# A relative-position table made in the first stage and spread over its rows head by head, DRAM to DRAM

## The chip, the cores and the metric

The kernel runs on one core of a Trainium2 chip. The metric is the time on the device in microseconds (us), from the start of the program to its end. The core has five engines that each run their own instruction stream in order: TensorE (PE in the profile, with PEld for its weight loads), VectorE (DVE), ScalarE (ACT), GpSimd (POOL) and SyncE (SP). SP computes nothing here and issues most DMA transfers; POOL issues the rest. The transfers of both run on 16 shared DMA engines.

## What is computed

One inference step of a hybrid encoder layer, for a prompt of 512 frames and a sample of 64 frames with a cache of 1024 past frames. A projection of 18,032 columns feeds two branches, a gated delta rule over 16 heads and a sparse attention over 16 heads, which are gated, summed and projected back. The change touches only the bias that the attention adds to its logits, which depends on the head and on the distance between key and query:

```python
def sparse_attention(q, qi, wi, q_pos, K, V, KI, topk, rel_bias):
    ...
    rel = top_idx - q_pos[None, :, None]
    bias = rel_bias[rel_bucket(rel)].astype(jnp.float32)
    ...
    logits = jnp.where(valid[:, :, None, None, :], logits + bias, -jnp.inf)
    p = jax.nn.softmax(logits, axis=-1).astype(V.dtype)
```

`rel_bias` has 32 buckets by 16 heads. Distances beyond 128 all fall in one bucket, so a head needs 384 distinct values at most near the diagonal.

## The kernel before

A Python class records the whole program by hand. The weight matrices are cut into **tiles** of 128 columns by 2048 rows; `run_tile` (L314) handles tile n: 64 matmuls with the high part of the weights (`whi`), then 32 with the low part (`wlo`), 96 in all, of 128x288 each. During tile n, `split` (L276) makes `whi` and `wlo` of tile n+1: ACT writes the rounded weights and their negative, then two POOL-issued transfers add the raw weights (`wraw`) onto `wlo` in flight. At the 84th matmul, `load` (L264) has SP issue the 1 MB load of `wraw` for tile n+3; it waits until the transfers that read the buffer's former content have landed.

The program has stages. In the first one (until about 410 us) the first projections, the indexer's scores and the start of the top-k run. Then comes the **delta-rule stage** (until about 1619 us), with four to six tiles for each of its 16 heads: `head_pre(h)` (L1260) opens head h ahead of its key tile. `open_att` (L1775) starts the **attention stage**, two tiles per head (queries `qb`, gate `zb`). Two stages for the output follow.

All work besides the tiles (decays, triangular solve, scan, attention of a head, stores) is written as generators, called tasks. `spawn` starts one; after each matmul of a tile, `tick` (L156) steps each task that is due and so writes its next instructions between the tile's matmuls. When a task is due is decided while the program is written, by a planner that keeps a clock for PE, one for each engine and one for DMA, and a time at which each tensor is ready. On the chip nothing of this clock is left but the order of the instructions on each engine, with waits on semaphores. For a transfer the planner advances its DMA clock by bytes that it works out from the shapes of the operands `aps`:

```python
        for x in aps:
            m = 1
            for s in x.shape[1:]:
                m *= s
            n = max(n, m)
        ...
            by = 4 * n * out.shape[0]
            self.dma = max(self.dma, start + 1500) + by / 360.0
            end = self.dma + 1300
```

A matmul advances the PE clock at least to the time when its operands are ready (`account_pe`, L123), and tasks that wait for a tensor are due when the planner holds it ready.

**The bias.** `bias_setup` (L1278) is a task of the attention stage. It loads three small constants (`oh`, `rb`, `far`), makes the table `f` of 16 heads by 512 distances with one matmul (`biasp`), and writes it to DRAM as `d_F` of 16 x 128 x 384: 128 equal rows for each head, 3 MB in one transfer from 16 partitions. A read of `d_F` at a row pitch of 383 instead of 384 (`toeplitz`, L1301) then gives a head's block of 128 queries by 256 keys, shifted by one from row to row. `attend` (L1340) reads this block into `BT` for its head, once the tasks `kv_load` and `bias_setup` are done; `attend_block` adds it to the logits `lg`, in blocks named `L`. Ahead of the first head, `conv_out` (L1306) transposes four pieces (`nc`), copies them to `ncr` and stores them, and `kv_load` transposes the cached keys (`kst`, `kcp`). `gate_vectors` (L1510) loads `gada`, 64 pieces of 256 KB, through the whole attention stage.

Of the kernel before, what the change touches and what calls it, by code (L numbers as in the profile page):

```python
# [7 lines left out]
F32 = mybir.dt.float32  # L8
# [200 lines left out]
class Kern(Plan):  # L209
# [138 lines left out]
    def consts(self, ctx):  # L348
        nc, tc, i = self.nc, self.tc, self.i
        cp = self.cp = ctx.enter_context(tc.tile_pool(name="cp", bufs=1))  # L350
        self.ident = cp.tile([128, 128], F32, name="ident")
        self.A.dma_start(self.ident, i["k_ident"])
        self.mE = cp.tile([128, 2, 128], F32, name="mE")
        self.ones = cp.tile([128, 1], F32, name="ones")
        self.V.memset(self.ones, 1.0)
        self.pm = ctx.enter_context(tc.tile_pool(name="pm", bufs=3, space=PSUM))
        self.px = ctx.enter_context(tc.tile_pool(name="px", bufs=2, space=PSUM))
        self.pc = ctx.enter_context(tc.tile_pool(name="pc", bufs=2, space=PSUM))
        self.po = ctx.enter_context(tc.tile_pool(name="po", bufs=1, space=PSUM))
        self.dp = ctx.enter_context(tc.tile_pool(name="dp", bufs=1, space=DRAM))  # L360
        dt = self.dp.tile
        self.d_g = dt([16, TX], F32, name="d_g")
        self.d_kT = dt([2, 128, T], F32, name="d_kT")
        self.d_v = dt([T, 256], F32, name="d_v")
        self.d_oa = dt([H, 128, T], F32, name="d_oa")
        self.d_za = dt([H, 128, T], F32, name="d_za")
        self.d_gb = dt([H, 128, T], F32, name="d_gb")
        self.d_t = dt([2, KO, 128, T], F32, name="d_t")
        self.d_ya = dt([KO, 128, T], F32, name="d_ya")
        self.d_F = dt([16, 128, 384], F32, name="d_F")  # L370
        self.d_D = [dt([128, T], F32, name=f"d_D{e}") for e in range(2)]

# [887 lines left out]
    def head_pre(self, h):  # L1260
        def pre():
            if h == 0:
                self.join(self.misc_task)
            if h >= 3:
                self.join(self.heads[h - 3]["scan"])
            st = self.heads[h] = dict(h=h)
            st["dec"] = self.spawn(self.decays(st))
            st["scan"] = self.spawn(self.scan(st))
        return pre
# [7 lines left out]

    def bias_setup(self):  # L1278

        i, p, V, S = self.i, self.p3, self.V, self.S  # L1280
        oh = p.tile([32, 512], F32, tag="L3", name="oh", bufs=1)
        S.dma_start(oh, i["k_onehot"])
        rb = p.tile([32, 16], F32, name="rb", bufs=1)
        S.dma_start(rb, i["rel_bias"])
        self.far = p.tile([128, 16], F32, name="far", bufs=1)
        S.dma_start(self.far, i["rel_bias"][15:16, :].partition_broadcast(128).rearrange("p a b -> p (a b)"))
        yield [oh, rb, self.far], 9000
        ps = yield from self.tr("biasp")
        self.mm(ps[:16, :], rb, oh)
        f = p.tile([16, 512], F32, tag="PT3", name="bf", bufs=1)  # L1290
        V.tensor_copy(f, ps[:16, :])
        self.fars = p.tile([128, 8], F32, name="fars", bufs=1)
        v = self.far.rearrange("p (a b) -> p a b", b=2)
        for s in range(2):
            V.tensor_copy(self.fars[64 * s:64 * s + 64, :], v[64 * s:64 * s + 64, :, s])
        yield [f]

        S.dma_start(self.d_F, f[:, 0:384].unsqueeze(1).to_broadcast([16, 128, 384]))
        yield [self.d_F]

    def toeplitz(self, h, n, w):  # L1301

# [36 lines left out]

    def attend(self, a):  # L1340
        S, p, h = self.S, self.p3, a["h"]
        yield from self.wait(self.kv_task, self.bias_task)
        BT = p.tile([128, 256], F32, tag="BT", name=f"BT{h}")
        S.dma_start(BT, self.toeplitz(h, 128, 256))
        yield [BT, a["qT"], a["zt"]]
        yield from self.wait(*[self.spawn(self.attend_block(a, t, BT)) for t in (3, 2, 1, 0)])
        if h % 2:
            a["sample"] = self.spawn(self.attend_sample(h // 2))
# [426 lines left out]
    def open_att(self):  # L1775
        self.drain()
        self.c2.close()
        self.c3, self.p3 = self.pool("p3")
        self.slack = 0.0
        self.gpool = lambda: self.p3  # L1780
        self.bias_task = self.spawn(self.bias_setup())
        self.spawn(self.conv_out())
        self.spawn(self.gate_vectors())
        self.qb_pre(0)()
# [41 lines left out]
    def run(self):  # L1826
        tc = self.tc
        with ExitStack() as ctx:
            ctx.enter_context(tc.manual_schedule())
            self.consts(ctx)  # L1830
            cp = self.cp
# [3 lines left out]
                setattr(self, n, cp.tile([128, 5, 16], F32, name=n))  # L1835
            self.gate = cp.tile([128, KO, 2], F32, name="gate")
            self.diag = cp.tile([128, 64], F32, name="diag")
            self.ur = cp.tile([128, 32], F32, name="ur")
            self.heads, self.att, self.kvT, self.tok = {}, {}, {}, {}
            self.score_tasks, self.topk_task = [], None  # L1840
# [9 lines left out]
            p = self.p1  # L1850
# [7 lines left out]
            for b in range(2):  # L1858
                q = p.tile([128, 2, 128], F32R, name=f"qss{b}", bufs=1)
                self.V.tensor_scalar(q, self.ident.unsqueeze(1).to_broadcast([128, 2, 128]), 0.0, None, op0=ALU.mult)  # L1860
                self.qss.append(q)
            self.tri = p.tile([128, 2, 128], F32, name="tri", bufs=1)
            self.cache_task = self.spawn(self.cache_idx())
            self.load(3)
            for n in range(2):
# [70 lines left out]
```

## Time and profile before

| | us |
|---|---|
| runs | 3054.83, 3056.27, 3066.11 |
| median of the runs | 3056.27 |
| the profiled execution, its own time | 3063.92 |
| its span in the trace | 3061.8 |

| busy share of the span | |
|---|---|
| PE | 96% |
| PEld | 92% |
| ACT | 50% |
| DVE | 39% |
| POOL | 13% |

The page shows 40 slices of the span. PE is at 9 tenths or more in nearly all of them; the exceptions are the first two, the slices at about 1620 to 1700 us (7 and 8 tenths) and some in the output stages. The DMA engines carry 183 GB/s on average. To read it: PE bounds the kernel nearly everywhere, so a stretch in which PE stands idle can be won, and work elsewhere costs only where PE comes to wait for it.

### The profile page before, as it was taken

The numbers are of one execution on the slowest core, as the hardware profiler recorded it, in microseconds if no ns is written. First come the engines' busy times: TensorE is split into PE (matmuls) and PEld (weight loads), VectorE is DVE, ScalarE is ACT, GpSimd is POOL, SyncE is SP. The second block draws the span as 40 slices with busy tenths as digits, with TensorE's granted clock in tenths as the row PEclk, the third lists the DMA queues.
The fourth block names the chain that finished last, engine by engine and source line by source line (L and its number), as shares of the span: only waits on it lengthen the run. The fifth ranks groups of instructions, "written<-read, shape, count | busy, mean of one in ns | idle before, by whom it ended". The sixth has DMA issues, their size and how long they took to land.

```text
span 3061.8 us, 59253 instructions
## 1 busy us (share of the span) xinstructions
PE 2934.6 (96%) x23931; PEld 2814.4 (92%) x23931; DVE 1204.6 (39%) x3643; ACT 1533.3 (50%) x3428; POOL 391.5 (13%) x776
## 2 busy tenths in 40 slices
PE   6999999999999999999997899999999999999897
PEld 2599999999999999999996899899999899999897
DVE  3344996545455545545531444244412111111112
ACT  3266444556555565555552455355445444444454
POOL 1011111111111111111110001111011111111110
PEclk7999999999999999999998999999999999999999
DMA  9875877677677766676678776777769998888875
GB/s 330 272 160 128 198 184 182 157 163 161 160 163 161 164 159 153 151 172 153 156 160 172 167 169 166 182 169 169 167 152 255 236 232 220 208 215 214 222 160 141
DMA packets 572387, 558.81 MB, mean 183 GB/s; under 512 B 54865, under 2 KB 467426, under 8 KB 570898
## 3 DMA queue, kind: packets, MB, share of 16 engines
q1 hardware_dynamic: 517826, 357.81, 41.3%
q0 software_dynamic: 54144, 197.16, 34.0%
q8 instruction: 188, 3.08, 0.4%
q14 instruction: 85, 0.70, 0.1%
q10 hardware_dynamic: 144, 0.07, 0.0%
HBM read 310.37 MB, written 47.45 MB: 117 GB/s over the span
## 4 chain that ended last, share of the span: by engine, by line
PE 82%; DMA 9%; DVE 3%; ACT 3%; SPq 2%; issue 1%; POOL 0%; ACTq 0%; DVEq 0%; POOLq 0%
PE mm L221 67%; SPq L58 2%; DMA za<-d_za 1%; DMA wlo<-wraw 1%; PE ada L221 1%; PE ob L221 1%; DMA gbl<-d_gb 1%; PE lg L221 1%; PE mmp L221 1%; PE dot L221 1%; PE po L221 1%; DMA xf<-in_x_sample 1%; DMA wa<-in_w_ada 1%; ACT whi L58 1%; ACT wlo L58 1%
## 5 line engine op out<-in xcount | busy, mean ns | idle before, releaser
L221 PE MATMUL mm<-hh,whi 128*128 128x288 f32 (+1 forms) x4448 | 1217.2, 300 | 4.8 <-ACT gth L58 4.5
L221 PE MATMUL mm<-hl,whi 128*128 128x288 f32 (+1 forms) x4448 | 1215.9, 300 | 0.0
L221 PEld LDWEIGHTS mm<-hh,whi 128*128 128x128 f32 (+1 forms) x4448 | 837.8, 188 | 14.0 <-ACT gth L58 5.3
L221 PEld LDWEIGHTS mm<-hl,whi 128*128 128x128 f32 (+1 forms) x4448 | 837.8, 188 | 7.9 <-issue 3.8
L221 PE MATMUL mm<-hh,wlo 128*128 128x288 f32 (+1 forms) x4448 | 683.0, 302 | 4.5 <-DMA wlo<-wraw 4.5
L221 PEld LDWEIGHTS mm<-hh,wlo 128*128 128x128 f32 (+1 forms) x4448 | 615.6, 190 | 6.6 <-DMA wlo<-wraw 4.7
L58 POOL DMA_DIRECT2D wlo<-wraw x376 | 324.0, 862 | 2313.2 <-ACT wlo L58 1926.8
L58 ACT ACTIVATE whi<-wraw 128x512 fp32r<-128x512 f32 x756 | 467.4, 619 | 98.1 <-DMA wraw<-in_w_branch_b 63.1
L58 ACT ACTIVATE wlo<-whi 128x512 fp32r<-128x512 f32 x752 | 475.2, 632 | 76.4 <-PE mm L221 35.9
L221 PE MATMUL mm<-ga,whi 128*128 128x288 f32 x1024 | 142.4, 299 | 7.5 <-DVE ta L58 7.5
L221 PEld LDWEIGHTS mm<-ga,whi 128*128 128x128 f32 x1024 | 139.7, 192 | 8.4 <-DVE ta L58 8.4
L221 PE MATMUL mm<-mg,whi 128*128 128x288 f32 x1024 | 143.6, 297 | 0.0
L221 PE MATMUL mm<-gb,whi 128*128 128x288 f32 x1024 | 138.8, 296 | 0.3 <-DVE tb L58 0.3
L221 PEld LDWEIGHTS mm<-mg,whi 128*128 128x128 f32 x1024 | 138.2, 189 | 0.0
L221 PEld LDWEIGHTS mm<-gb,whi 128*128 128x128 f32 x1024 | 136.8, 188 | 0.6 <-DVE tb L58 0.5
L58 DVE SCALAR_TENSOR_TENSOR cv<-raw,cw,cv 128x579 f32<-128x579 f32 x144 | 117.8, 818 | 33.6 <-ACT cv L58 30.4
L58 DVE SCALAR_TENSOR_TENSOR gacc<-gada,cs,gacc 128x512 f32<-128x512 f32 x120 | 86.7, 744 | 30.9 <-DMA gada<-in_w_ada 30.8
L58 ACT ACTIVATE raw<-mm 128x288 f32<-128x288 f32 x96 | 36.8, 383 | 87.4 <-PE mm L221 86.6
L58 ACT ACTIVATE gth<-mm 128x288 f32<-128x288 f32 x64 | 25.9, 407 | 108.3 <-PE mm L221 104.6
L58 ACT ACTIVATE x<-px 128x128 f32<-128x128 f32 x80 | 22.0, 275 | 116.0 <-PE px L221 115.6
L58 DVE TENSOR_TENSOR xf<-yp,xf 128x512 f32<-128x512 f32 (+1 forms) x18 | 11.4, 632 | 160.5 <-PE yp L236 133.7
L58 DVE SCALAR_TENSOR_TENSOR tb<-tb,mm 128x288 f32<-128x288 f32 x32 | 14.5, 452 | 143.3 <-DMA tb<-d_t 110.3
(493 smaller groups left out, 3422.8 us busy)
## 6 DMA issues: line engine op xcount, KB each, us to landing
wlo<-wraw POOLq DMA_DIRECT2D x376, 512.0 KB, 5.5
wraw<-in_w_in SPq DMA_DIRECT2D x140, 1024.0 KB
wa<-in_w_ada SPq DMA_DIRECT2D x64, 512.0 KB
gada<-in_w_ada SPq DMA_DIRECT2D x64, 256.0 KB
wraw<-in_w_branch_a SPq DMA_DIRECT2D x16, 1024.0 KB
wraw<-in_w_branch_b SPq DMA_DIRECT2D x16, 1024.0 KB
wraw<-in_w_out SPq DMA_DIRECT2D x16, 1024.0 KB
d_t<-gth SPq DMA_DIRECT2D x32, 288.0 KB
```

The lines of the kernel that those rows point to most:

```text
L58: r = f(*a, **k)
L221: self.nc.tensor.matmul(out, lhsT, rhs, start=start, stop=stop, **k)
```

## The change

Four things change. The table `f` is made by a task of the first stage, from that stage's pool, with `far` and `fars` moved to the pool that lives throughout. What is written to DRAM from it is only `d_f`, 16 rows of 384 (24 KB). The 128 equal rows of a head are now written by `bias_rows(h)`, called in `head_pre(h)`: one transfer from DRAM to DRAM of 192 KB, issued by POOL, whose source is read 128 times. And `attend` no longer waits for the bias task.

```diff
--- before.py
+++ after.py
@@ -367,6 +367,7 @@
         self.d_gb = dt([H, 128, T], F32, name="d_gb")
         self.d_t = dt([2, KO, 128, T], F32, name="d_t")
         self.d_ya = dt([KO, 128, T], F32, name="d_ya")
+        self.d_f = dt([16, 384], F32, name="d_f")
         self.d_F = dt([16, 128, 384], F32, name="d_F")
         self.d_D = [dt([128, T], F32, name=f"d_D{e}") for e in range(2)]
 
@@ -1263,6 +1264,7 @@
                 self.join(self.misc_task)
             if h >= 3:
                 self.join(self.heads[h - 3]["scan"])
+            self.bias_rows(h)
             st = self.heads[h] = dict(h=h)
             st["dec"] = self.spawn(self.decays(st))
             st["scan"] = self.spawn(self.scan(st))
@@ -1277,26 +1279,28 @@
 
     def bias_setup(self):
 
-        i, p, V, S = self.i, self.p3, self.V, self.S
-        oh = p.tile([32, 512], F32, tag="L3", name="oh", bufs=1)
+        i, p, cp, V, S = self.i, self.p1, self.cp, self.V, self.S
+        oh = p.tile([32, 512], F32, name="oh", bufs=1)
         S.dma_start(oh, i["k_onehot"])
         rb = p.tile([32, 16], F32, name="rb", bufs=1)
         S.dma_start(rb, i["rel_bias"])
-        self.far = p.tile([128, 16], F32, name="far", bufs=1)
-        S.dma_start(self.far, i["rel_bias"][15:16, :].partition_broadcast(128).rearrange("p a b -> p (a b)"))
-        yield [oh, rb, self.far], 9000
+        far = self.far
+        S.dma_start(far, i["rel_bias"][15:16, :].partition_broadcast(128).rearrange("p a b -> p (a b)"))
+        yield [oh, rb, far], 3000
         ps = yield from self.tr("biasp")
         self.mm(ps[:16, :], rb, oh)
-        f = p.tile([16, 512], F32, tag="PT3", name="bf", bufs=1)
+        f = p.tile([16, 512], F32, name="bf", bufs=1)
         V.tensor_copy(f, ps[:16, :])
-        self.fars = p.tile([128, 8], F32, name="fars", bufs=1)
-        v = self.far.rearrange("p (a b) -> p a b", b=2)
+        v = far.rearrange("p (a b) -> p a b", b=2)
         for s in range(2):
             V.tensor_copy(self.fars[64 * s:64 * s + 64, :], v[64 * s:64 * s + 64, :, s])
         yield [f]
-
-        S.dma_start(self.d_F, f[:, 0:384].unsqueeze(1).to_broadcast([16, 128, 384]))
-        yield [self.d_F]
+        S.dma_start(self.d_f, f[:, 0:384])
+        yield [self.d_f]
+
+    def bias_rows(self, h):
+
+        self.G.dma_start(self.d_F[h], self.d_f[h:h + 1].unsqueeze(1).to_broadcast([1, 128, 384]))
 
     def toeplitz(self, h, n, w):
 
@@ -1339,7 +1343,7 @@
 
     def attend(self, a):
         S, p, h = self.S, self.p3, a["h"]
-        yield from self.wait(self.kv_task, self.bias_task)
+        yield from self.wait(self.kv_task)
         BT = p.tile([128, 256], F32, tag="BT", name=f"BT{h}")
         S.dma_start(BT, self.toeplitz(h, 128, 256))
         yield [BT, a["qT"], a["zt"]]
@@ -1778,7 +1782,6 @@
         self.c3, self.p3 = self.pool("p3")
         self.slack = 0.0
         self.gpool = lambda: self.p3
-        self.bias_task = self.spawn(self.bias_setup())
         self.spawn(self.conv_out())
         self.spawn(self.gate_vectors())
         self.qb_pre(0)()
@@ -1835,6 +1838,8 @@
                 setattr(self, n, cp.tile([128, 5, 16], F32, name=n))
             self.gate = cp.tile([128, KO, 2], F32, name="gate")
             self.diag = cp.tile([128, 64], F32, name="diag")
+            self.far = cp.tile([128, 16], F32, name="far")
+            self.fars = cp.tile([128, 8], F32, name="fars")
             self.ur = cp.tile([128, 32], F32, name="ur")
             self.heads, self.att, self.kvT, self.tok = {}, {}, {}, {}
             self.score_tasks, self.topk_task = [], None
@@ -1860,6 +1865,7 @@
                 self.V.tensor_scalar(q, self.ident.unsqueeze(1).to_broadcast([128, 2, 128]), 0.0, None, op0=ALU.mult)
                 self.qss.append(q)
             self.tri = p.tile([128, 2, 128], F32, name="tri", bufs=1)
+            self.bias_task = self.spawn(self.bias_setup())
             self.cache_task = self.spawn(self.cache_idx())
             self.load(3)
             for n in range(2):
```

**On SP, where the attention stage opens**, before (`d_t<-gth` is the last gate tile's store):

```order
L58 DMA d_t<-gth_19979 128x576
L58 DMA oh<-in_k_onehot 32x512
L58 DMA rb<-in_rel_bias 32x16
L58 DMA far<-in_rel_bias 128x16
L58 DMA gada_20017<-in_w_ada 128x512
L58 DMA gada_20019<-in_w_ada 128x512
L58 DMA KT_20023<-d_kT 128x576
```

and in the changed kernel:

```order
L58 DMA d_t<-gth_20000 128x576
L58 DMA gada_20042<-in_w_ada 128x512
L58 DMA gada_20044<-in_w_ada 128x512
L58 DMA KT_20048<-d_kT 128x576
L58 DMA V_20050<-d_v 128x4x128
```

The three loads of `bias_setup` are gone from between the store and the first `gada`.

In the same place, some fifteen transfers further on, where SP issues the read of the first head's block, before:

```order
L58 DMA wraw_20157<-in_w_in 128x16x128
L58 DMA gada_20162<-in_w_ada 128x512
L58 DMA d_F<-bf 2048x1x384
L58 DMA gada_20248<-in_w_ada 128x512
L58 DMA wraw_20296<-in_w_in 128x16x128
L58 DMA gada_20323<-in_w_ada 128x512
L58 DMA BT_20329<-d_F 128x256
L58 DMA gada_20435<-in_w_ada 128x512
```

and in the changed kernel:

```order
L58 DMA wraw_20182<-in_w_in 128x16x128
L58 DMA gada_20187<-in_w_ada 128x512
L58 DMA gada_20268<-in_w_ada 128x512
L58 DMA wraw_20313<-in_w_in 128x16x128
L58 DMA BT_20332<-d_F 128x256
L58 DMA gada_20345<-in_w_ada 128x512
L58 DMA gada_20423<-in_w_ada 128x512
```

The 3 MB write `d_F<-bf` is gone from between two `gada` loads, and `BT` stands one `gada` earlier.

**On POOL, where head 10 of the delta rule opens** (`raw` and `newc` are pieces of the convolution, `dd10` the first step of the head's decays, `wlo66` the low weights of the tile that follows), before:

```order
L58 MEMSET raw41_13468 128x3
L58 COPY raw41_13468<-cst_221 128x3
L58 MEMSET q9_13473 128x64
L58 MEMSET dd10_13500 64x64
L58 COPY newc_228<-raw41_13468 128x3 x2
L58 DMA wlo66_13506<-wraw66_13286 128x1024
L58 MEMSET ssq9_13553 64x1
L58 DMA wlo66_13506<-wraw66_13286 128x1024
```

and in the changed kernel:

```order
L58 DMA d_F_88<-d_f_87 128x1x384
L58 COPY newc_231<-raw41_13406 128x3 x2
L58 DMA wlo66_13450<-wraw66_13118 128x1024 x2
L58 MEMSET kd9_13571 64x128
L58 MEMSET vb9_13623 64x128
L58 MEMSET raw26_13647 128x3
L58 COPY raw26_13647<-cst_224 128x3
L58 MEMSET os8_13691 64x1
L58 COPY newc_231<-raw26_13647 128x3 x2
L58 DMA wlo67_13683<-wraw67_13414 128x1024 x2
L58 MEMSET k10_13832 128x64
L58 MEMSET dd10_13840 64x64
```

`d_F<-d_f` now stands ahead of the two `wlo66` transfers, and `dd10` has moved behind them and behind the next tile's `wlo67`, about one tile later.

**On PE, in the scan of the same head** (`px`, `pS`, `pks`, `po` are its steps; the two digits end the name: head 10, chunk 2 or 3; `mm` are matmuls of the tiles), before:

```order
L221 MATMUL pS102_0_15070<-x102_15054,kd10_14638 128x128
L221 MATMUL po102_15040<-x102_15054,e110_13604 128x128
L221 MATMUL mm71_0_14938<-hh_102,wlo71_14731 128x288 x3
L221 MATMUL mm71_1_14982<-hh_102,wlo71_14731 128x288 x8
L221 MATMUL pks103_0_15100<-S102_15073,k10_13893 128x128
L221 MATMUL po103_15099<-S102_15073,q10_14335 128x128
L221 MATMUL mm71_1_14982<-hh_102,wlo71_14731 128x288 x6
L221 MATMUL px103_0_15115<-r103_15103,TT10_13972 128x128
```

and in the changed kernel:

```order
L221 MATMUL pS102_0_15436<-x102_15407,kd10_14472 128x128
L221 MATMUL po102_15380<-x102_15407,e110_13953 128x128
L221 MATMUL mm73_0_15259<-hh_105,wlo73_15016 128x288
L236 MATMUL vbp11_0_15447<-ident_60,raw43_15170 128x128 x4
L221 MATMUL mm73_0_15259<-hh_105,wlo73_15016 128x288
L236 MATMUL vbq11_0_15457<-ident_60,raw43_15170 64x128
L221 MATMUL mm73_0_15259<-hh_105,wlo73_15016 128x288
L221 MATMUL mm73_1_15331<-hh_105,wlo73_15016 128x288 x3
L221 MATMUL pks103_0_15469<-S102_15439,k10_13832 128x128
L221 MATMUL po103_15468<-S102_15439,q10_14226 128x128
L221 MATMUL mm73_1_15331<-hh_105,wlo73_15016 128x288 x6
L221 MATMUL px103_0_15492<-r103_15472,TT10_14061 128x128
```

The scan runs two tiles later (`mm73` for `mm71`), and six matmuls of tiles and two groups of transposes stand between `pS102` and `pks103` where eleven matmuls stood.

## Rows read from the trace of the kernel before

**Rows 1.** The page: busy time by engine; the chain that ended last, by engine.

```profile
PE 2934.6 (96%) x23931; PEld 2814.4 (92%) x23931; DVE 1204.6 (39%) x3643; ACT 1533.3 (50%) x3428; POOL 391.5 (13%) x776
...
PE 82%; DMA 9%; DVE 3%; ACT 3%; SPq 2%; issue 1%; POOL 0%; ACTq 0%; DVEq 0%; POOLq 0%
```

**Rows 2.** Chain that ended last, longest pieces: start us, us, what.

```profile
1649.32 24.92 DMA wlo<-wraw
1674.86 14.94 SPq L58
1689.90 4.36 DMA BT<-d_F
...
2874.71 12.73 PE mm L221 x96
```

**Rows 3.** PE timeline, start of attention: start, us, what, xcount [idle before <-releaser].

```profile
1624.96 0.31 PE L236 MATMUL nc<-ident,newc 128*96 128x128 f32 x1 [3.47 <-DVE ncr L58]
...
1637.62 1.11 PE L236 MATMUL kcp<-ident,kst 128*128 128x128 f32 x4 [4.40 <-DVE ncr L58]
...
1644.48 1.03 PE L221 MATMUL biasp<-oh,rb 32*16 32x512 f32 x2
```

**Rows 4.** PE timeline, the first two attention heads.

```profile
1671.15 2.05 PE L221 MATMUL mm<-hh,wlo 128*128 128x288 f32 x7 [4.48 <-DMA wlo<-wraw]
...
1694.84 1.22 PE L221 MATMUL lg<-KT,qT 128*128 128x256 f32 x2 [19.11 <-DVE L L58]
...
1700.10 0.29 PE L221 MATMUL mm<-hh,whi 128*128 128x288 f32 x1
```

**Rows 5.** SP timeline, the same stretch: transfers as SP issues them.

```profile
1619.76 0.32 SPq L58 DMA_DIRECT2D d_t<-gth  x1
1624.36 0.35 SPq L58 DMA_DIRECT2D oh<-in_k_onehot  x1
...
1626.48 1.62 SPq L58 DMA_DIRECT2D gada<-in_w_ada  x2
...
1646.26 0.67 SPq L58 DMA_DIRECT2D d_F<-bf  x1
```

**Rows 6.** Stretches: busy us (xcount) of PE, PEld, DVE, ACT, POOL; PEclk, DMA share, GB/s.

```profile
1625.00:1630.00 5.00, 5.00 (x38) 4.97 (x39) 0.10 (x1) 0.00 (x0) 0.61 (x1) 1.00 1.11 171
...
1650.00:1655.00 5.00, 5.00 (x40) 5.00 (x39) 0.00 (x0) 0.00 (x0) 0.18 (x1) 1.00 0.89 101
...
1680.00:1685.00 5.00, 0.00 (x0) 0.00 (x0) 0.00 (x0) 0.00 (x0) 0.00 (x0) 0.50 0.89 103
```

**Rows 7.** Chain, pieces: after the second idle time, and in the next head.

```profile
1638.73 5.18 PE mm L221 x22
...
1725.34 4.49 PE mm L221 x34
```

**Rows 8.** PE timeline, the next head's first logits.

```profile
1722.11 1.67 PE L221 MATMUL lg<-KT,qT 128*128 128x512 f32 x4
```

**Rows 9.** Stretches: the first delta-rule heads, and the whole stage; columns as rows 6.

```profile
450.00:700.00 250.00, 249.27 (x2325) 244.27 (x2324) 140.78 (x459) 142.24 (x331) 39.10 (x104) 1.00 0.72 165
450.00:1619.00 1169.00, 1152.80 (x11036) 1123.00 (x11035) 583.25 (x2100) 672.70 (x1611) 179.56 (x509) 1.00 0.70 161
```

**Rows 10.** Waits of PE in the delta-rule stage, the largest: total us, times, longest.

```profile
PE kdq L236 <- DVE T L58: 4.4, 3, 1.8
```

**Rows 11.** DMA issues of the delta-rule stage: KB each, median us to landing.

```profile
wlo<-wraw POOLq DMA_DIRECT2D x144, 512.0 KB, 5.0
```

**Rows 12.** POOL timeline, end of the delta-rule stage: the second wlo issue of a tile.

```profile
1600.41 0.86 POOL L58 DMA_DIRECT2D wlo<-wraw  x1 [2.97 <-ACT wlo L58]
```

**Rows 13.** PE timeline: the first matmuls that read this wlo.

```profile
1614.88 4.41 PE L221 MATMUL mm<-hh,wlo 128*128 128x288 f32 x32
```

**Rows 14.** SP timeline, first stage.

```profile
149.13 3.49 SPq L58 DMA_DIRECT2D cik<-in_cache_idx_k  x2
```

**Rows 15.** PE timeline, first stage: the first matmuls that read cik.

```profile
158.74 0.63 PE L236 MATMUL cikp<-ident,cik 128*128 128x128 f32 x4
```

## The prediction

> **What bounds the kernel now.** I began with the busy times: PE works for 96% of the span, and 82% of the chain that ended last is PE's own [rows 1]. So only time in which PE stands still, or runs slowly, can be won. The chain's longest pieces that aren't PE's stand close together, at about 1650 to 1694 us [rows 2]; that is why the attention stage's opening was read next, engine by engine.
>
> PE's timeline shows two short waits there for `ncr`, 3.47 and 4.40 us [rows 3], and two others, 4.48 us for a `wlo` transfer and 19.11 us for the block `L` on DVE [rows 4]. DVE is only the last link of the long one: it adds `BT`, whose read the chain has at 1689.90, landing 4.36 us later [rows 2]. What kept `BT`? SP issued `d_F<-bf` at 1646.26 [rows 5], 3 MB read from 16 partitions. In the windows after it the DMA engines are 0.89 busy and move only 101 GB/s, and still 103 GB/s while PE is idle, against 171 GB/s before it began [rows 6]. At 101 GB/s, 3.15e6 bytes take 31 us. The `wlo` transfer issued in that time landed after 24.92 us, SP stood for 14.94 us at a `gada`, and only then came `BT` [rows 2]; a `wlo` transfer of the delta-rule stage lands in 5.0 us [rows 11]. [...]
>
> **The change part by part: what the attention stage gains.**
> 1. Three loads leave SP between the store of `d_t` and the first `gada`: 1626.48 - 1624.36 = 2.12 us [rows 5]. The store of `nc` that `kst`'s PE work follows stands behind them; so the wait of 4.40 us at `kcp` becomes 2.28. Gain 2.12 (from 0, if DVE's own chain ends last there, to 2.12).
> 2. Behind that wait 22 matmuls took 5.18 us [rows 7]. One costs 12.73 / 96 = 0.1326 us in an undisturbed run [rows 2], so 22 cost 2.92, and 2.26 us went into a lowered clock. After the wait of 3.47 us the window at 1625 still has clock 1.00 [rows 3, 6]; after 2.28 I expect it too. Gain 2.26 (bound: 0).
> 3. `biasp` leaves the stage, 1.03 us [rows 3].
> 4. The wait for `wlo` goes: 4.48 [rows 4].
> 5. The wait for `BT` goes: 19.11 [rows 4]. Next late would be `BT`'s own landing, 4.36 us [rows 2]; its read now stands one `gada` earlier on SP, so I count nothing.
> 6. From 1671.15 to 1700.10 are 28.95 us, of which 19.11 are waiting; the other 9.84 hold 32 matmuls of the tile and 8 `lg` [rows 4]. At full clock these are 32 x 0.1326 = 4.24, and for 8 `lg` 2.57: the next head spends 1725.34 - 1722.11 = 3.23 us on 8 `lg` with 5 tile matmuls between, 5 x 0.1326 = 0.66 of it [rows 7, 8]. So 9.84 - 6.81 = 3.03 is the lowered clock's.
>
> Sum: 2.12 + 2.26 + 1.03 + 4.48 + 19.11 + 3.03 = **32.0 us**. Only 1 and 2 are soft; without them 27.7.
>
> **What the first stage pays.** `biasp` costs its 1.03 us again, where PE has nothing idle to hide it. The three loads stand on SP before others: 2.1 us by the same rows. Behind them comes `cik`, issued from 149.13 to 152.62 [rows 14] and, with a landing of some 5 us as for `wlo` [rows 11], ready at 157.6; its reader starts at 158.74 [rows 15]. Of the 2.1 us, 1.1 lies in that slack and 1.0 at most is paid: I take 0.5. `f` and `d_f` have a thousand microseconds until they are first read late, and some 250 until head 0 opens.
>
> **What the delta-rule stage pays.** Two things, neither of which the trace of before shows.
>
> *The row writes.* Sixteen transfers of 196,608 bytes. Their price from the nearest rows: at the 101 GB/s of the same bytes written from 16 partitions [rows 6], 1.95 us of all 16 engines; at the 171 GB/s of mixed traffic [rows 6], 1.15; twice 1.95, if reading DRAM as well doubles it, 3.9. The same rows of 1,536 bytes are written, so I take 1.95: 31 us in a stage of 1169 us at a DMA share of 0.70 [rows 9], which becomes 0.73. On POOL one more issue per head, 0.86 us as for a `wlo` transfer [rows 12], 14 us on an engine that works 180 of 1169 us [rows 9]. Behind it on POOL's queue stand the two `wlo` transfers of the tile. Their cover: the second one's issue at 1600.41 [rows 12] + 5.0 [rows 11] = 1605.4, first read at 1614.88 [rows 13]; 9.5 us are spare. A write of 2 to 4 us plus 0.86 us of issue fits in. Nothing waits for the write itself until `BT`. Cost on the path: 0 (up to 1).
>
> *The order.* The planner sizes the new transfer from the source operand: n = 128 x 384 = 49,152, times 4 x 128 rows = 25.2 MB, 69.9 us of its DMA clock. The true 192 KB would be 0.5 us; the old write, with 16 partitions, was sized right. After each head's opening its clock for DMA, and through the next `wlo` also that for PE, is tens of microseconds late; tasks count as due that on the chip are not. The order shows this: head 10's `dd10` has moved a tile later, and its scan two tiles. Does PE then wait? The stage's whole idle time is now 1169 - 1152.8 = 16.2 us [rows 9], and its longest single waits are 1.8 us [rows 10], so chain steps stand with hardly more work between them than they need. At the quoted place, seven tile matmuls and two groups of transposes stand where eleven matmuls stood. I compared this distance for all 384 gaps between chained steps: only 16 are shorter than the shortest of their kind before, by 0.2 to 1.06 us, 6.5 us in all. And the last head's output ends 11 instead of 126 tile matmuls ahead of the attention stage, which may cost a microsecond or two. Against this, early heads were nearly free of waits, 0.73 us in 250 [rows 9]. I take 2.5 us; bounds -5 (part of the 16.2 goes, since other gaps get longer) and +15 (the 6.5 doubled, and the stage's end).
>
> [...]
>
> **Sum.** -32.0 + 1.0 + 0.5 + 0 + 2.5 = -28.0 us. The profiled execution took 3063.92 us, its span 3061.8; it becomes 3035.9. The median of the runs is 7.65 us lower, 3056.27; the same gain gives **3028**.
>
> **The rivals.**
> - *Part of the long wait stays.* `BT` now follows a 1 MB `wraw` in SP's order. For: that order. Against: the next heads read `BT` in such traffic without a wait of this size. If 8 us of the 19.11 stay, about 3036.
> - *The wait wasn't `d_F`'s.* `BT` comes as late for another reason, the 4.48, 19.11 and 3.03 stay, and only 2 + 2 + 1 - 1 - 0.5 - 2.5 are left: about 3055. For: the DMA engines are full before 1646 as well, 1.11 in the window at 1625 [rows 6]. Against: the 101 GB/s begin with the write and end with `BT`'s issue.
> - *The row writes overrun their cover.* If DRAM to DRAM costs over 9.5 us in place of 2 to 4, PE waits for `wlo` after each head's opening: at 11.4 us, 1.9 x 16 = 30 us, and the gain is gone, about 3058. For: source and target are both DRAM, and one row is read 128 times. Against: it would be a fifth of the 101 GB/s at hand.
> - *Slower: the false clock leaves each head's chain bare.* Decays that begin a tile later reach the scan's first steps without cover; PE waits at each of the 16 heads. From (28.0 + 2.5 + 15.3) / 16 = 2.9 us a head the kernel is measurably slower; at 4 us, 64 - 30.5 = +33, about 3090. For: the moved rows at head 10. Against: the 384 gaps, of which 16 shrank.
>
> **How the numbers follow.** This kernel's measurement tells 0.5%, 15.3 us, from no change. Forecast 0.74; its own range goes from 3021 (-5 in place of 2.5) to 3043 (+15 and terms 1 and 2 gone in part). The first rival 0.06, the second 0.05, the third 0.09, the slower one 0.06. Faster is the forecast and nearly all of the first rival, less its upper tail: 0.79; same 0.14; slower 0.07. The range 3015 to 3047 leaves out the third and the slower rival, most of the second, and little of the forecast.
>
> **What would show it.** Right: in the timeline `kcp` waits some 2.3 us; no wait for `wlo` or `L` of more than 2 us between 1650 and 1710; the first `qb` tile has clock 1.00; no window there near 101 GB/s with a share of 0.9. In the delta-rule stage the row write lands in 3 to 5 us, `wlo` still in about 5, and PE's idle time between 450 us and the attention stage is 14 to 25 us. Wrong: PE waiting for `wlo` right after a head opens (third rival), for DVE's or ACT's steps of decays and scan with over 40 us in all (the slower one), or at the attention stage for the last head's output; a first-stage wait at `cikp` of over 2 us; or an `L` that still waits for `BT`.

## The result, and the profile after

| | us |
|---|---|
| kernel before, median | 3060.28 |
| changed kernel, median (runs 3036.28 to 3039.12) | 3037.93 |
| ratio to before, 95% interval | 0.9931 (0.9913 to 0.9948) |
| ratio in a second series, 95% interval | 0.9917 (0.9897 to 0.9937) |
| the profiled execution's span, before and after | 3061.8 and 3035.6 |

Predicted were 3028 and a range of 3015 to 3047. The change is faster by 0.5 to 0.9%, and the time lies in the range. But the gain is 22 us where 28 were forecast, and the experiments show that two terms were off by about 12 us each, one for the change and one against it. That the sum came out near is luck.

What was forecast for the attention stage's opening is there. PE's timeline of the changed kernel, all its idle times from 1600 to 1720 us (columns as in rows 3):

```profile
1626.42 0.45 PE L236 MATMUL nc<-ident,newc 128*96 128x128 f32 x1 [4.82 <-DVE ncr L58]
...
1637.63 0.66 PE L236 MATMUL kcp<-ident,kst 128*128 128x128 f32 x4 [0.75 <-DVE ncr L58]
```

Of the four waits of rows 3 and 4, the long two are gone, `kcp` is down from 4.40 to 0.75 and `nc` up from 3.47 to 4.82. That is 5.57 us of waiting in place of 31.46: 25.9 less, with 25.7 forecast. SP's timeline and three windows of the same stretch (rows 5 and 6):

```profile
1620.99 0.42 SPq L58 DMA_DIRECT2D d_t<-gth  x1
1625.94 0.81 SPq L58 DMA_DIRECT2D gada<-in_w_ada  x2
...
1652.60 1.92 SPq L58 DMA_DIRECT2D BT<-d_F  x1
```

```profile
1625.00:1630.00 5.00, 3.58 (x15) 3.50 (x16) 0.48 (x2) 0.00 (x0) 0.71 (x1) 0.50 1.07 222
1650.00:1660.00 10.00, 10.00 (x75) 9.76 (x74) 2.23 (x4) 5.43 (x10) 0.92 (x2) 1.00 0.82 212
1660.00:1670.00 10.00, 10.00 (x72) 9.23 (x71) 6.97 (x27) 4.55 (x13) 0.80 (x1) 1.00 0.70 149
```

No `d_F` write from 16 partitions and no window near 101 GB/s with the engines 0.9 busy is left; `BT` is read at 1652.60 instead of 1689.90. One thing went otherwise: the granted clock, at 1.00 in the window at 1625 before, is now 0.50 there, behind the wait of 4.82 us. In the kernel before it was 0.50 some 11 us later, behind the wait of 4.40, as this window of before shows:

```profile
1638.00:1643.00 5.00, 5.00 (x23) 5.00 (x22) 2.55 (x5) 0.41 (x1) 0.00 (x0) 0.50 0.45 122
```

What it costs is seen in the two transposes `nc` and the 19 tile matmuls that follow that wait, from the start of the first `nc` to the start of the matmul behind them, before and then after:

```profile
1624.96:1627.74 2.78, 2.78 (x22) 2.75 (x22) 0.14 (x1) 0.00 (x0) 0.65 (x1) 1.00 1.05 197
```

```profile
1626.42:1631.39 4.97, 4.97 (x22) 4.89 (x22) 0.14 (x1) 0.00 (x0) 0.00 (x0) 0.51 1.03 227
```

The same work takes 2.2 us more.

The delta-rule stage, first before and then after, with the waits and DMA issues after (columns as in rows 9 to 11):

```profile
410.00:1600.00 1190.00, 1173.80 (x11194) 1144.00 (x11194) 617.52 (x2163) 685.90 (x1634) 184.92 (x530) 1.00 0.70 162
```

```profile
410.00:1600.00 1190.00, 1181.58 (x11220) 1155.45 (x11219) 617.85 (x2148) 680.49 (x1617) 194.19 (x549) 1.00 0.72 165
```

```profile
PE z L221 <- ACT TT L58: 4.5, 7, 1.0
PE px L221 <- DVE r L58: 1.4, 2, 0.9
```

```profile
wlo<-wraw POOLq DMA_DIRECT2D x151, 512.0 KB, 5.2
...
d_F<-d_f POOLq DMA_DIRECT2D x16, 192.0 KB, 5.4
```

PE is idle for less than before, 8.4 us (1190.00 - 1181.58) against 16.2 (1190.00 - 1173.80). The row write lands in 5.4 us, `wlo` in 5.2, and no wait of PE for `wlo` is among those of the stage. So no cover was overrun.

Where the time went, by the starts of the same three tiles in PE's timeline, of the kernel before and then of the changed one:

```profile
163.06 0.30 PE L221 MATMUL mm<-hh,whi 128*128 128x288 f32 x1
...
1619.12 0.30 PE L221 MATMUL mm<-hh,whi 128*128 128x288 f32 x1
...
1716.16 0.29 PE L221 MATMUL mm<-hh,whi 128*128 128x288 f32 x1
```

```profile
165.48 0.29 PE L221 MATMUL mm<-hh,whi 128*128 128x288 f32 x1
...
1619.22 0.30 PE L221 MATMUL mm<-hh,whi 128*128 128x288 f32 x1
...
1685.62 0.30 PE L221 MATMUL mm<-hh,whi 128*128 128x288 f32 x1
```

| stretch | before | after | difference |
|---|---|---|---|
| start to the second tile whose output is `mm` | 163.06 | 165.48 | +2.4 |
| from there to the attention stage's first tile, 92 tiles | 1456.06 | 1453.74 | -2.3 |
| from there over four tiles of the opening | 97.04 | 66.40 | -30.6 |
| from there to the end of the span | 1345.64 | 1349.98 | +4.3 |

The sum is -26.2, the difference of the spans. The second and fourth rows are the odd ones: half of the waits vanished in the second, and yet little was won, and the fourth grew though the change gives it no new work. One cause is that PE's own work takes some 0.4% longer, which no view of waits shows. But these are two single executions, and such stretches differ by several us from one to the next: the fourth takes from 1341.6 to 1355.4 us in the kernels below, and the shortest of these has the changed kernel's slower matmuls. Only the third row is far outside of that. The longest unbroken run of matmuls in the first stage, from the chain that ended last (start, us, what), first of the kernel before, then of the changed one:

```profile
325.70 114.50 PE mm L221 x864
```

```profile
328.70 115.73 PE mm L221 x868
```

114.50 / 864 = 132.5 ns before; 115.73 / 868 = 133.3 ns after, at the same granted clock of 1.00. That is 0.08 us per tile of 96, in each of the 141 tiles that stream `hh` and `hl` and the 16 that stream `gb`: some 12 us, most of them in the table's second and fourth rows.

### The profile page after: what moved, and what is told of

Read it like the earlier page. It is cut to its first block, busy times and chain, and to the rows that moved or that the text cites. A ratio compares the mean times of both kernels' runs of the same rounds, so it can differ in the third digit from the quotient of the medians.

```text
span 3035.6 us, 59288 instructions
## 1 busy us (share of the span) xinstructions
PE 2938.0 (97%) x23931; PEld 2824.9 (93%) x23931; DVE 1205.0 (40%) x3643; ACT 1531.8 (50%) x3428; POOL 399.3 (13%) x792
## 4 chain that ended last, share of the span: by engine, by line
PE 82%; DMA 10%; ACT 3%; DVE 2%; SPq 2%; issue 1%; POOL 0%; ACTq 0%; DVEq 0%; POOLq 0%
PE mm L221 66%; DMA yl<-d_ya 2%; SPq L58 2%; DMA za<-d_za 2%; DMA wlo<-wraw 1%; DMA wa<-in_w_ada 1%; DMA gbl<-d_gb 1%; PE ob L221 1%; PE lg L221 1%; PE ada L221 1%; PE po L221 1%; PE mmp L221 1%; PE dot L221 1%; DMA xf<-in_x_sample 1%; ACT wlo L58 1%
## 5 line engine op out<-in xcount | busy, mean ns | idle before, releaser
L58 ACT ACTIVATE gth<-mm 128x288 f32<-128x288 f32 x64 | 25.9, 407 | 103.7 <-PE mm L221 102.5
```

Of the source, the lines that this page charges most:

```text
L58: r = f(*a, **k)
```

## The experiments

The changed kernel ran once more, beside three of those below:

> The changed kernel once more, beside the next three on one chip: ratio to the kernel before 0.993 as in its first runs (interval 0.991 to 0.995), matmul interval 133.3 ns.

Measured: 0.9917 (0.9897 to 0.9937), 133.3 ns.

**The matmul's interval.** `far` and `fars` moved to the pool that lives throughout, 64 + 32 bytes per partition. Behind them in memory come `hh` and `hl`, which stream through PE in each of the 141 tiles: `hh` moved from address 23072 in its partition, 32 modulo 128, to 23168, 0 modulo 128, and `hl` and `gb` likewise. (Addresses are those of the built programs.) The first experiment adds 32 unused bytes.

```diff
             self.fars = cp.tile([128, 8], F32, name="fars")
+            self.pad = cp.tile([128, 8], F32, name="pad")
             self.ur = cp.tile([128, 32], F32, name="ur")
```

> The changed kernel with one unused tile of 32 bytes per partition behind fars, so that the activations hh and hl (the operand that streams through PE) begin at an address that is 32 modulo 64 again, as in the kernel before, instead of 0. Every instruction and its order stay. Theory A (the address sets the matmul's interval: 132.5 ns before, 133.3 ns in the changed kernel wherever hh, hl or gb stream, equal where ga and mg stream, whose address did not move): interval back to 132.5 ns, 15072 matmuls x 0.83 ns = 12.5 us off 3038, so about 3025.5. Rival B (the interval belongs to the execution or the chip, not to the kernel): 3038, with an interval of 133.3 ns as likely as before.

Measured: 3028.71 us, ratio 0.9883 (0.986 to 0.9906), by the ratios 10 to 15 us below the two series of the changed kernel. Its longest run of matmuls, in the same view:

```profile
328.40 115.13 PE mm L221 x868
```

115.13 / 868 = 132.6 ns. A is borne out here. The same 32 bytes in the kernel before:

```diff
+            self.pad = cp.tile([128, 8], F32, name="pad")
             self.ur = cp.tile([128, 32], F32, name="ur")
```

> The kernel before with the same unused 32 bytes, which moves hh, hl and gb from 32 to 0 modulo 64 and changes no instruction. Theory A: interval 133.3 ns, +12.5 us, ratio to the kernel before 1.004, about 3072. Rival B: ratio 1.000.

Measured: ratio 1.0001 (0.9988 to 1.0014), 132.6 ns (114.60 us for 864). So "0 modulo 64" was wrong: `hh` stood at 23104, which is 64 modulo 128, and ran as before. The next one, with 96 unused bytes (`[128, 24]` in the same line), gives `hh` the changed kernel's own address.

> The kernel before with 96 unused bytes per partition, which put hh, hl and gb at the very addresses of the changed kernel (hh at 23168, a multiple of 128; 32 unused bytes put it at 23104, 64 modulo 128, and the interval stayed at 132.5 ns). No instruction changes. Theory A2 (a streaming operand that begins at a multiple of 128 costs 0.83 ns more per matmul): interval 133.3 ns, +12.5 us, ratio 1.004. Rival B2 (something else of the changed kernel sets it): 132.5 ns, ratio 1.000.

Measured: ratio 1.0025 (1.001 to 1.004), 3 to 12 us slower with no instruction changed; the run of matmuls:

```profile
330.28 115.19 PE mm L221 x864
```

133.3 ns: A2 holds for the interval, with a price of 7.7 us by the ratio, under the 12.5 computed. Last, 96 unused bytes ahead of the weights instead, in the kernel before:

```diff
+        self.wpad = ctx.enter_context(tc.tile_pool(name="wpad", bufs=1, side="right")).tile([128, 24], F32, name="wpad")
         self.wp = ctx.enter_context(tc.tile_pool(name="wp", bufs=2, side="right"))
```

> The kernel before with 96 unused bytes on the other side of the memory: the weights whi and wlo and the operands ga and mg now begin at multiples of 128, hh, hl and gb stay at 32 modulo 128. No instruction changes. Theory A2 (the streaming operand's address decides): 132.5 ns where hh, hl and gb stream, 133.3 where ga and mg stream. Rival L (the weights' address, or both): 133.3 ns everywhere.

This kernel ran once, in 3075.48 us, so its time says little. PE's timeline of two output stages, a group of 64 matmuls on `ga` and one on `gb`, each with the group that follows it:

```profile
2577.78 8.64 PE L221 MATMUL mm<-ga,whi 128*128 128x288 f32 x64
2586.26 4.40 PE L221 MATMUL mm<-ga,wlo 128*128 128x288 f32 x32
...
2679.85 8.69 PE L221 MATMUL mm<-gb,whi 128*128 128x288 f32 x64
2688.39 4.43 PE L221 MATMUL mm<-gb,wlo 128*128 128x288 f32 x32
```

From start to start, `ga` takes (2586.26 - 2577.78) / 64 = 132.5 ns and `gb` (2688.39 - 2679.85) / 64 = 133.4; `hh` too has 133.3 in this kernel (115.20 us for 864). A2 has it the wrong way round at both places, and L is wrong for `ga`. With the weights at a multiple of 128, `ga`, itself at a multiple of 128, is fast, and `hh` and `gb`, at 32, are slow. In the kernel before the weights and `ga` both begin at 96 modulo 128, and a tile of 96 matmuls on `ga` takes 2593.71 - 2580.99 = 12.72 us, 132.5 ns each:

```profile
2580.99 8.64 PE L221 MATMUL mm<-ga,whi 128*128 128x288 f32 x64
...
2593.71 8.64 PE L221 MATMUL mm<-ga,whi 128*128 128x288 f32 x64
```

All combinations that were run, addresses modulo 128:

| streaming operand | weights | ns per matmul | seen in |
|---|---|---|---|
| 32 | 96 | 132.5 to 132.6 | before, first experiment |
| 64 | 96 | 132.6 | second |
| 96 | 96 | 132.5 | `ga` in the kernel before |
| 0 | 96 | 133.3 | changed kernel, third |
| 32 | 0 | 133.3 to 133.4 | fourth, `hh` and `gb` |
| 0 | 0 | 132.5 | fourth, `ga` |

Two rules fit all six: it is slow where exactly one of the two begins at a multiple of 128, or where the streaming operand begins 32 bytes behind the weights, modulo 128. No run separates them, and why the addresses matter is open.

**The order in the delta-rule stage.** First the changed kernel with the planner not told of the row writes; then the kernel before with nothing but the planner's wrong charge.

```diff
     def bias_rows(self, h):
-        self.G.dma_start(self.d_F[h], self.d_f[h:h + 1].unsqueeze(1).to_broadcast([1, 128, 384]))
+        self.G.eng.dma_start(self.d_F[h], self.d_f[h:h + 1].unsqueeze(1).to_broadcast([1, 128, 384]))
```

> The changed kernel, but the planner is not told of the sixteen row writes, so that in the delta-rule stage PE has exactly the order of the kernel before; the row writes stand at the same heads. Activations at 0 modulo 64 as in the changed kernel. Theory C (the shifted order happened to save waits: PE idle in the stage 16.2 us before, 8 to 9 after): idle time back at about 16 us, 6 to 8 us slower than the changed kernel, about 3045. Rival D (the shift is neutral or costs, and the idle time saved is chance between executions): 3035 to 3039.

```diff
                 self.join(self.heads[h - 3]["scan"])
+            start = max(self.t.get("pool", 0.0), self.pe)
+            self.t["pool"] = start + 60
+            self.dma = max(self.dma, start + 1500) + 4 * 49152 * 128 / 360.0
             st = self.heads[h] = dict(h=h)
```

> The kernel before, with nothing of the change but the planner's wrong charge: at each head's opening its DMA clock is put 69.9 us ahead. PE's order in the delta-rule stage is then exactly that of the changed kernel; no row writes, the 3 MB write stays. Theory C (the later, shifted order saves waits): PE idle in the stage some 8 us in place of 16, about 8 to 11 us faster than before, ratio 0.9965 to 0.9975. Rival D (the row writes or chance did it): ratio 1.000. Rival of the prediction (the false clock leaves chains bare): slower, ratio 1.001 or more.

Measured: 0.9957 (0.994 to 0.9973) for the first, by the ratios 8 to 12 us slower than the changed kernel's two series; 0.9969 (0.9957 to 0.9982) for the second, 9.5 us faster than before. The same stretch of the first, then of the second, and the second's largest wait in the stage (columns as above):

```profile
410.00:1600.00 1190.00, 1172.16 (x11139) 1142.44 (x11138) 615.19 (x2149) 679.16 (x1613) 193.24 (x544) 1.00 0.71 163
```

```profile
410.00:1600.00 1190.00, 1181.36 (x11241) 1154.70 (x11240) 615.09 (x2151) 684.78 (x1633) 185.78 (x531) 1.00 0.70 163
```

```profile
PE z L221 <- ACT TT L58: 4.6, 7, 1.0
```

With the order of before, PE is idle for 17.8 us, with the shifted one for 8.6, and the waits for `kdq` of rows 10 are gone, as in the changed kernel. The other profiles agree: in this window PE is idle for 14.4 to 20.2 us in the kernels that have the order of before and write nothing else there, and for 8.4 to 10.7 in all that have the shifted one. Of the first, the waits at the attention stage's opening:

```profile
PE kcp L236 <- DVE ncr L58: 4.4, 1, 4.4
PE nc L236 <- DVE ncr L58: 2.8, 1, 2.8
```

C is shown: the wrong charge saves about 9 us (5 to 13 by the interval) by itself. In this second kernel the 3 MB write still stands at the attention stage, and its waits with it; of the two for `ncr` only that of `nc` is left:

```profile
PE lg L221 <- DVE L L58: 16.5, 1, 16.5
PE mm L221 <- DMA wlo<-wraw: 5.2, 2, 3.1
PE nc L236 <- DVE ncr L58: 4.5, 1, 4.5
```

**The row writes.** The table early, but written at once from 16 partitions in the first stage:

```diff
-            self.bias_rows(h)
...
-        S.dma_start(self.d_f, f[:, 0:384])
-        yield [self.d_f]
+        S.dma_start(self.d_F, f[:, 0:384].unsqueeze(1).to_broadcast([16, 128, 384]))
+        yield [self.d_F]
```

> The table early as in the changed kernel, but written in the first stage as one transfer of 3 MB from 16 partitions, with no row writes; the delta-rule stage has the order of the kernel before. Theory E (that transfer takes its 31 us at 101 GB/s wherever it stands and holds up a wlo transfer by some 20 us, of which 9.5 are covered): a wait of PE of about 10 us between 160 and 220 us, 10 us or more slower than e3_rows_free. Rival F (there is cover enough in the first stage): within 2 us of e3_rows_free, and then the split into rows buys nothing. The waits of 4.48 and 19.11 us in the attention stage are gone by both.

Measured: 3071.95 us, ratio 1.0025 (1.001 to 1.004), 20 us over the kernel with row writes in the same order (0.9957). E is shown. A window of it, and the two largest waits of PE between 100 and 420 us:

```profile
175.00:185.00 10.00, 10.00 (x77) 10.00 (x76) 2.13 (x6) 3.22 (x8) 0.00 (x0) 1.00 0.88 101
```

```profile
PE gcp L221 <- DVE g L58: 10.8, 1, 10.8
PE mm L221 <- DMA wlo<-wraw: 8.0, 2, 5.9
```

101 GB/s at a DMA share of 0.88, as in rows 6, and PE stops for `wlo` and then for `g`, which DVE makes from a small load (`dtb`) that SP issued behind the write, in two parts at 165.53 and 174.45 us; from 185 to 200 us DVE did nothing. In the delta-rule stage this kernel, without row writes, leaves PE idle for 15.1 us (busy 1174.91 of 1190.00); with them it was 17.8. Both lie in the 14.4 to 20.2 us of the kernels without row writes, so a cost of the sixteen isn't told from that spread. Then three more row writes for each head, to a second buffer:

```diff
...
+        for _ in range(3):
+            self.G.eng.dma_start(self.d_F2[h], self.d_f[h:h + 1].unsqueeze(1).to_broadcast([1, 128, 384]))
```

> The kernel with the order of e3_rows_free, but each head writes its rows four times (three times to a second buffer that nothing reads), all on POOL's queue ahead of the two wlo transfers. One row write lands in 5.4 us in the changed kernel. Theory G (a row write takes 2 to 4 us of the DMA engines, and 9.5 us of cover hide it): three more take 6 to 12 us per head, so between nothing and 3 us per head come to light, 0 to 45 us over e3_rows_free; 16 us taken. Rival H (the row writes already cost PE time in e3_rows_free, as one more thing behind which wlo waits): the whole 6 to 12 us per head come to light, 96 us or more.

Measured: 1.0094 (1.0076 to 1.0112), 42 us over the same order with one write each, 2.6 us a head. The time is within G, but not for its reason alone. The three write the same place, so the program has each wait for the one ahead of it, and POOL with it; from the waits of the delta-rule stage:

```profile
POOL d_F L1306 <- DMA d_F<-d_f: 184.6, 31, 7.8
...
PE u L221 <- DVE Z L58: 21.2, 3, 9.1
```

POOL stood for 184.6 / 16 = 11.5 us a head. PE's largest new waits are for steps of the triangular solve (`Z`), and none is for `wlo`; what ties them to POOL is open. Last, the rows written all at once: by POOL where head 0 opens, by POOL where the attention stage opens, and there by SP as one transfer. In all three the call in `head_pre` is replaced and the planner is not told of the writes.

```diff
-            self.bias_rows(h)
+            if h == 0:
+                for g in range(H):
+                    self.bias_rows(g)
```

> As e3_rows_free (order of the kernel before in the delta-rule stage), but all sixteen row writes stand together on POOL where head 0 opens, at about 410 us. Theory I (what matters is that the rows are written before the attention stage; 3 MB from DRAM to DRAM in one go hold up a wlo transfer once): at 2 to 4 us each, 31 to 64 us of transfers and the two wlo transfers behind them, of which 9.5 us are covered: PE waits 20 to 50 us once, ratio to e3_rows_free 1.007 to 1.016, about 3072 to 3100. Rival J (DRAM to DRAM is so fast that the burst is hidden): within 3 us of e3_rows_free.

```diff
-            self.bias_rows(h)
...
+        for h in range(H):
+            self.bias_rows(h)
         self.spawn(self.conv_out())
```

> As e3_rows_free, but the sixteen row writes stand on POOL where the attention stage opens, before anything else of it; the table is early. Theory I: the gain of the attention stage is taken back by 31 to 64 us of transfers there, time as in the kernel before or up to 30 us over it, 3060 to 3095. Rival K (only the write from 16 partitions was slow, or only the three loads mattered): within 5 us of e3_rows_free, 3047 to 3057.

```diff
-            self.bias_rows(h)
...
+        self.S.eng.dma_start(self.d_F, self.d_f.unsqueeze(1).to_broadcast([16, 128, 384]))
         self.spawn(self.conv_out())
```

> As e10_late_rows, but the rows of all heads are written by one transfer of 3 MB from DRAM to DRAM that SP issues where the attention stage opens; before, one transfer of 3 MB from 16 partitions of SBUF stood on the same queue. Theory M (the 16 partitions as source made it slow): about 300 GB/s as for the sixteen row writes of e10_late_rows, 10 to 15 us, time within 5 us of e10_late_rows. Rival N (one transfer over SP's queue, or its shape of 16 x 128 x 384, made it slow): a stretch near 101 GB/s of some 30 us with SP and the wlo transfers held up, and 15 us or more over e10_late_rows.

Measured: 0.9974 (0.9963 to 0.9985), 0.9976 (0.9966 to 0.9986) and 0.9958 (0.9939 to 0.9976), against 0.9957 (0.994 to 0.9973) head by head. Theory I fails: no 20 to 50 us come back. The first two lie 5 to 6 us above the spread-out writes, which the intervals don't separate from none. The stretch of the writes in the second and in the third, in the columns of rows 6:

```profile
1620.00:1625.00 5.00, 5.00 (x40) 5.00 (x39) 0.00 (x0) 0.41 (x1) 3.32 (x7) 1.00 1.04 206
1625.00:1630.00 5.00, 2.55 (x20) 2.29 (x18) 0.00 (x0) 4.50 (x9) 2.72 (x6) 1.00 0.99 294
1630.00:1635.00 5.00, 0.00 (x0) 0.00 (x0) 0.00 (x0) 0.51 (x1) 2.99 (x5) 0.60 1.05 329
```

```profile
1630.00:1635.00 5.00, 1.81 (x11) 1.57 (x10) 0.48 (x2) 3.70 (x7) 1.72 (x2) 0.86 1.10 367
1635.00:1640.00 5.00, 5.00 (x32) 4.92 (x32) 0.00 (x0) 0.00 (x0) 0.00 (x0) 0.79 1.07 270
1640.00:1645.00 5.00, 3.40 (x26) 3.17 (x24) 0.00 (x0) 0.00 (x0) 0.00 (x0) 1.00 1.04 317
```

With the rows among other traffic the engines move 206 to 329 GB/s and 270 to 367, not 101. The packet records of the traces give the write's own time: its 2048 packets of 1,536 bytes run from 1647.6 to 1688.7 us in the kernel before, 41 us, from 167.5 to 202.3 with the early 3 MB, 35 us, and from 1632.1 to 1645.8 in the third of these, 13.7 us; the sixteen transfers of the second run from 1622.8 to 1637.3, 14.4 us. A burst still has a price in its place: in their profiles the first has one wait of 7.5 us for `k`, the second one of 17.5 us for `ncr` and the third 9.3 and 3.2, where the spread-out kernel has 4.4 and 2.8. M holds: the same 3 MB over the same queue take 13.7 us in place of 41 when their source is DRAM. The slow part was the source, not the size, the queue or the moment. A source in SBUF alone doesn't make it so: in the trace of before, stores of 288 KB from 128 partitions (`d_t`, `d_oa`, `d_za`) go through in 1.6 us, 184 GB/s, at the median of 38, and one of their packets of 2,304 bytes takes 99 ns on average, where one of 1,536 bytes from the 16 partitions takes 200. No run wrote the same 3 MB from other partitions, so what in a source of 16 partitions is slow is not shown.

## Why the prediction was right, and where it was not

- **What bounded the opening** was right. Before's 3 MB write was the cause of the waits for `wlo` and `L`; they go when it goes or becomes fast, and stay when only the order changes (16.5 and 5.2 us). Forecast 32.0 us, measured 30.6 (30.9 without the longer interval). In three more profiles with the old write (the kernel before with unused bytes) the four tiles take 94.45 to 96.89 us, in two more with the new ones (the second series, 32 unused bytes) 67.17 and 66.46: a gain of 27 to 31 us. The 31 us for the write itself were too few: its packets ran for 41.
- **Terms 1 and 2** failed, and were half made up for by the order. `nc` and `kcp` together wait for 5.2 to 7.9 us with the three loads (the kernel before, as it was and with unused bytes) and for 7.2, 8.7 and 8.5 without them in the same order (the planner not told, the early 3 MB, the burst at head 0). So no gain is seen from the loads' leaving, where term 1 had 2.12. The shifted order alone has 4.5 us, all at `nc`; the changed kernel has that order and 5.57. Term 2 gave nothing, as the lowered clock (0.50 in the window at 1625) moved to `nc` with the wait: 2.2 us lost there, where 2.26 were to be won. Of the 4.38 us of both terms some 2.4 came, by the order; the bound of 0 that each of them had was nearer.
- **The first stage** paid `biasp`'s 1.03 us and a wait of 0.6 at `cikp`, in the bounds given. The 2.4 us of the table say no more than that: its tile starts at 161.5 to 167.6 us in the five profiles with the first stage of before, and at 162.5 to 168.2 in the eight with that of the changed kernel.
- **The row writes** cost nothing that the traces tell from the spread, forecast 0 to 1, but the row that I took was the wrong one. The nearest row by bytes, 101 GB/s, was that of a source in 16 partitions; with a source in DRAM under way the engines moved 206 to 367 GB/s, two to three and a half times as much. The cover of 9.5 us was not overrun, and the split by heads that it was computed for brings no gain clear of the intervals. A row write landed in 5.4 us among other traffic; in the burst at the attention stage it was 6.9 us at the median, but the sixteen were issued in 13 us and their landings overlapped. One transfer of 3 MB and sixteen of 192 KB took 13.7 and 14.4 us and cost the same within the intervals.
- **The order** is the step that failed most: +2.5 us forecast, bounds -5 to +15, measured -9.5, and the 14 to 25 us of idle time that were to show the forecast right are 8.4. I counted the gaps that got shorter and took the 16.2 us of idle time as nearly given. The gaps that got longer were not priced against the rows of waits that they could remove, `kdq`'s 4.4 us to begin with.
- **The address** was missing from the sum: +12 us by the interval, 8 to 15 by the medians of the runs with unused bytes. The diff showed 96 bytes more in the pool ahead of `hh`; I gave moved tiles no price.

So in these two profiles -30.6 in the opening, +2.4 in the first stage, about -9.7 by the order and about +12 by the interval make -26.2; the forecast had -32.0, +1.5 and +2.5. The time is in the range because the order's error and the missing address nearly cancel, which is luck. The first two rivals fail with the waits for `L` and `wlo`, which are gone; the slower one fails with the order's sign. The third is far off: three more writes a head do cost PE time, but in its waits for `Z`, not for `wlo` as that rival had it.

The best kernel of this study is the changed one with 32 unused bytes: 3028.71 us, ratio 0.9883 (0.986 to 0.9906).

## What to carry to other kernels

Read a transfer's rate, not its size: 3 MB from 16 partitions were 41 us on the DMA engines, and the same bytes from DRAM 13.7, at a cost of 6 us or less, by the medians, at each of three places. When a change adds or moves a tile, compare the interval of an undisturbed run of matmuls in both traces before the rest is explained, since a few bytes can shift the operands of all of them: 96 did here, and the interval went from 132.5 to 133.3 ns. And where a new instruction enters a planner's accounts, price the gaps that get longer as well as those that shrink.

## What the runs showed of the hardware

- The same matmul of 128x288 takes 132.5 or 133.3 ns by the addresses of its operands (the granted clock was 1.00 in the runs of matmuls of the kernel before and the changed one): with (streaming operand, weights) modulo 128 bytes in their partitions, 133.3 to 133.4 at (0, 96) and (32, 0), 132.5 to 132.6 at (32, 96), (64, 96), (96, 96) and (0, 0). No other combination was run.
- While a write from 16 partitions of SBUF to DRAM was under way, in rows of 1,536 bytes, windows at both places where it stood show 101 GB/s in all with the DMA engines 0.88 to 0.89 busy; with the same rows from DRAM to DRAM under way they moved 206 to 367 GB/s, other traffic included, from POOL's queue and from SP's. The 3 MB took 41 and 35 us from the 16 partitions and 13.7 to 14.4 from DRAM; stores of 288 KB from 128 partitions moved at 184 GB/s at the median.
